# gMLP and SwiGLU layer: x loaded into y's rows, mod_w of g2 read in the v step, LN1 spread row by row, xT of two blocks as one tile, transposes one u step earlier

## The chip, the core and the metric

One core of a Trainium2 chip runs the whole layer as one program. The metric is the device time of the program in microseconds (us). PE is the matrix engine, DVE the vector engine, ACT the scalar engine, POOL the general engine; SP is the sequencer that issues nearly all DMA transfers of this kernel, one after the other, each when its waits are met. A kernel's time is the median of its runs. A bank is one PSUM bank, 128 partitions x 512 float32.

## The reference

One layer on x of 2048 rows x 1024 columns, float32:

```python
mod = silu(c) @ mod_w + mod_b                      # sh1, sc1, g1, sh2, sc2, g2: 1024 numbers each
h   = x * (1 + sc1) + sh1
u, v = split(gelu(h @ w_in + b_in), 2)             # 1024 columns each
v   = layer_norm(v)                                # times ln_g, plus ln_b
sv  = einsum('gts,bnsgc->bntgc', w_s * tril, v) + b_s   # within chunks of 128 rows, 8 groups of columns
x   = layer_norm(2 ** 0.25 * x + (1 + g1) * ((u * sv) @ w_out))           # LN1
h   = x * (1 + sc2) + sh2
g, u = split(h @ ffn_w_in, 2)                      # 2816 columns each
x   = layer_norm(2 ** 0.25 * x + (1 + g2) * ((silu(g) * u) @ ffn_w_out))  # LN2
```

## The kernel before

The 2048 rows are four blocks of 512 (TB), each of four tiles of 128 rows (NT). `mixer(sb)` takes blocks 2sb and 2sb+1 through the first half of the layer; it runs twice. Then `ffn_in(0)`, `ffn_in(1)` and `ffn_out` do the second half. Every float32 operand of a large product is split by `parts` (L91) into a rounded value, which ACT writes (L94), and a remainder, which DVE writes (L95); three matmuls (`HL`) make one product.

A mixer has three steps. **v** (L307 to L324): 384 matmuls of 128x512 for v, in two passes of 8 banks over 8 k steps; with each k step of the first pass `h_piece` loads the rows of x transposed (`xT`, two tiles of 128x512, one a block) and scales them; `wv_piece` loads the weight into a buffer of pool `xs`. The two passes end in sums into `vrow`, eight tiles of pool `late`. **u** (L376 to L383): 8 steps of 48 matmuls; step i also runs the jobs listed for ("u", i), and some of the spatial products (L359). **y** (L439 to L460): a Strassen form of the output product, seven products of 4 k steps of 12 matmuls, 336 in all, in the order 1, 2, 6, 5, 7, 3, 4. Each k step needs a left operand (`y_S`, in the 8 buffers of pool `hB`) and a right one (`y_T`, a 512 KB load from DRAM into the 6 buffers of pool `w`, L404). `evacuate` adds the banks up in `rows`, eight tiles of `late`: `with_x` (L410) loads a half row tile of x, 256 KB, into `xs` and DVE computes ALPHA x + bank (L415). `norm` (L431) then does LN1 of a block: four multiplications by ln1g (L434), the root on POOL (L183), four by 1/std plus ln1b (L435), and a store to DRAM (`x1d`). `norm(0)` stands at the end of product 3; `norm(1)`, of the second block, is run by the caller: for the first mixer in step ("v", 0, 0) of the second, for the second between the products of `ffn_in(0)`.

The u steps of the second mixer carry the *tails* of the first: `tail_load` reads x1d back (`x1c`, pool `late`), PE transposes it (`h2T`, L483), `h2_part` makes up to five operands of it, and `hop` stores put them into DRAM (L475). Tail i is the job of step ("u", i), so tail 7 belongs to the last u step. `load_ops` (L512) reads such operands for `ffn_in`: A11 and A12 in `following`, after the last u step, S1 and S2 after the mixer, S3, A22 and S4 inside `ffn_in`. Products 1, 2, 5, 6, 7, 4, 3 of `ffn_in` need A11, A12, S1, S2, S3, A22, S4 in turn; their weights (`f_0g_b` and so on, L543) go through `parts` as `f_0g_w`.

`mods(to, k, plus)` gives eight jobs `mod_col`: load a 512 KB tile of mod_w (`modw`, pool `lt`, 3 buffers), one DVE pass with a sum (L119), one small addition. sh2 and sc2 are read in steps ("v", 1, d) of the second mixer, g2 in its u steps 6 and 7. `spread` (L139) writes the eight columns of g2 to a line in DRAM, 4 bytes apiece (`g_bc_line`), and loads it back onto all partitions.

The order of each engine's instructions is fixed when the program is built: the tile framework schedules them by a model of time (L906), so a job may come earlier or later than where the code names it. On the chip each engine runs its list in that order.

Of the kernel before, what the change touches and what calls it, by code (L numbers as in the profile page):

```python
# [37 lines left out]
def gmlp_swiglu_layer(  # L38
# [237 lines left out]
    def mixer(sb, jobs, u_done):  # L276
# [8 lines left out]
        def h_piece(d):  # L285
            if sc1[d] is None:
                mod_of(sh1, 0, d, 0.0, "lt")()
                mod_of(sc1, 1, d, 1.0, ("lc", "bc")[d % 2])()
            for x, b in enumerate(blocks):
                r = new("lt" if sb else "u", f"xT{b}_{d}", HALF)  # L290
                nc.sync.dma_start(out=r, in_=xT[d, :, b * TB : (b + 1) * TB])
                nc.scalar.activation(r, r, AF.Identity, bias=sh1[d], scale=sc1[d])
                h[x][d] = parts(r, f"h{b}_{d}", ("hA", "hB")[x])

        def wv_piece(y, k):
            r = new("xs", f"wv{sb}_{y}{k}_raw", HALF)
# [107 lines left out]
            nc.sync.dma_start(out=w.bitcast(F32), in_=wot[B_OF[pr]][k])  # L404
            return w

        rows = [[new("late", f"r{b}_{t}") for t in range(NT)] for b in blocks]
        sts = [[stats_tile(f"ln1_{b}_{t}") for t in range(NT)] for b in blocks]

        def with_x(x, t, cs, ps):  # L410

            xt = new("xs", f"x{blocks[x]}_{t}{cs.start}", HALF)
            row = blocks[x] * TB + t * P
            nc.sync.dma_start(out=xt, in_=inp_x[row : row + P, cs])
            nc.vector.scalar_tensor_tensor(out=rows[x][t][:, cs], in0=xt, scalar=ALPHA, in1=ps, op0=ALU.mult, op1=ALU.add)  # L415

        def evacuate(pr, j, ps):
            if pr in (1, 6, 7, 4):
# [9 lines left out]
                if p == pr:  # L428
                    bn(rows[x][j], sts[x][j], y)

        def norm(x):  # L431
            for t, (mu, rs, nm) in enumerate(norms_of(sts[x], f"ln1_{blocks[x]}")):
                r = rows[x][t]
                nc.vector.scalar_tensor_tensor(out=r, in0=r, scalar=mu, in1=env["ln1g"], op0=ALU.subtract, op1=ALU.mult)  # L434
                nc.vector.scalar_tensor_tensor(out=r, in0=r, scalar=rs, in1=env["ln1b"], op0=ALU.mult, op1=ALU.add)  # L435
                nc.sync.dma_start(out=x1d[blocks[x]][t * P : (t + 1) * P, :], in_=r)
# [2 lines left out]
        order = (1, 2, 6, 5, 7, 3, 4)  # L439
        made = ahead([lambda pr=pr, k=k: (left_y(pr, k), right_y(pr, k)) for pr in order for k in range(NK)], 3)  # L440
        z = None
        for pr in order:
            if pr in (1, 2, 5):
                ps = [bank(f"y{sb}_{pr}_{j}") for j in range(4)]
                if pr == 1:
                    chain = ps
                if pr == 5:
                    z = ps
            ps = chain if pr in (1, 6, 7, 4) else z if pr == 3 else ps
            for k in range(NK):  # L450
                a, w = next(made)
                for j in range(4):
                    for part, wpart in HL:
                        nc.tensor.matmul(  # L454
                            ps[j], lhsT=a[:, part, j * P : (j + 1) * P], rhs=w[:, wpart, :],
                            start=(k == 0 and part == 0 and wpart == 0 and pr in (1, 2, 5)), stop=(k == NK - 1 and part == 1),
                            skip_group_check=True,
                        )
            for j in range(4):
                evacuate(pr, j, ps)  # L460
            if pr == 3:
                norm(0)
# [325 lines left out]
    def mods(to, k, plus):  # L788
        return [mod_of(to, k, d, plus) for d in range(ND)]
# [20 lines left out]
        jobs["u", k + 1] = [wo_prep(k)]  # L810
    jobs["u", 6] = [rows_of_ln1]
    norm = mixer(0, jobs, lambda: None)
    jobs = {("v", 0, 0): [norm]}
    for d, f in enumerate(zip(mods(sh2, 3, 0.0), mods(sc2, 4, 1.0))):
        jobs["v", 1, d] = f
    x1s = {}

    def x1_ahead(i):
        x1s[i] = tail_load(i // 4, i % 4, "late")

    jobs["v", 1, 6] += (lambda: x1_ahead(0),)
    for i in range(2 * NK):
        jobs["u", i] = [lambda i=i: tail(i // 4, i % 4, "lt", ["xs", "lt"], x1s[i])]
        if i < 2 * NK - 1:
            jobs["u", i].append(lambda i=i: x1_ahead(i + 1))
    jobs["u", 6] += mods(g2, 5, 1.0)[:NK]
    jobs["u", 7] += mods(g2, 5, 1.0)[NK:]

    def following():
        early.close()  # L830
        env["ops"] = phase("right", opsA11=(4, UNIT), opsA12=(4, UNIT), raw2=(4, ROW), hr=(1, UNIT))
        ops.update(load_ops(0, ("A11", "A12")))

# [76 lines left out]
```

## Time and profile before

| what | us |
|---|---|
| median of 3 runs | 1896.32 (1894.59 to 1896.58) |
| profiled execution, its own time | 1897.97 |
| its span in the trace | 1896.3 |
| PE busy | 1829.6 (96%) |
| DVE busy | 1251.6 (66%) |
| ACT busy | 687.5 (36%) |
| POOL busy | 513.7 (27%) |

In the trace the first mixer runs to 294 us, the second from 300 to 606, `ffn_in` from 607 to about 1475, `ffn_out` from there to the end. In a row of a timeline the number in brackets is the idle time of the engine before the first of the instructions and what ended it; "xN" is how many instructions of one kind follow each other.

### The profile page before, as it was taken

What the parts mean: (1) busy time and instruction counts of PE and PEld (TensorE: products, weight loads), DVE (VectorE), ACT (ScalarE), POOL (GpSimd) and SP (SyncE); (2) the same over time, 40 slices, a digit from 0 to 9 for tenths busy, and PEclk for the clock granted to TensorE, in tenths of its full rate; (3) what the DMA queues carried; (4) which work ended last, traced back from release to release, by engine and by line L of the source; (5) the groups of instructions that cost most, each with busy time, mean ns of one, the idle gap of its engine ahead of it and who ended that gap; (6) DMA issues with size and microseconds to landing.
All of it is one profiled execution on the core that took longest, in us unless ns stands there. A gap on an engine that the chain in (4) does not pass through costs nothing.

```text
span 1896.3 us, 23225 instructions
## 1 busy us (share of the span) xinstructions
PE 1829.6 (96%) x8168; PEld 1513.0 (80%) x8168; DVE 1251.6 (66%) x1785; ACT 687.5 (36%) x1132; POOL 513.7 (27%) x327
## 2 busy tenths in 40 slices
PE   7999998999977999999999999999999999999997
PEld 5888877888755788888888888888888888888886
DVE  7658759555966776776765656677766344455858
ACT  4254324163421344543333333333334333333320
POOL 0000001001110465576444653555453000000104
PEclk9999999999988999999999999999999999999998
DMA  9638667536988846753567646445645665556532
GB/s 380 198 125 309 199 217 275 195 121 223 366 298 241 309 168 227 260 189 140 192 202 275 237 139 210 167 161 187 207 167 184 211 194 189 183 167 190 173 120 100
DMA packets 173319, 393.24 MB, mean 207 GB/s; under 512 B 20209, under 2 KB 36625, under 8 KB 173202
## 3 DMA queue, kind: packets, MB, share of 16 engines
q1 hardware_dynamic: 173138, 391.73, 59.8%
q8 instruction: 64, 1.05, 0.2%
q14 instruction: 53, 0.43, 0.1%
q0 software_dynamic: 64, 0.03, 0.0%
HBM read 266.11 MB, written 125.58 MB: 207 GB/s over the span
## 4 chain that ended last, share of the span: by engine, by line
PE 86%; DVE 4%; issue 4%; DMA 3%; ACT 1%; POOL 0%; SPq 0%; DVEq 0%; ACTq 0%; POOLq 0%
PE o L672 21%; PE u_ps L348 8%; PE v_ps L314 8%; PE y L454 4%; PE s_ps L359 1%; PE f_4g_X L530 1%; PE f_3g_X L530 1%; PE f_5g_X L530 1%; PE f_2g_X L530 1%; PE f_2u_X L530 1%; PE f_1u_X L530 1%; PE f_4u_X L530 1%; PE f_3u_X L530 1%; PE f_5u_X L530 1%; PE f_6g_X L530 1%
## 5 line engine op out<-in xcount | busy, mean ns | idle before, releaser
L672 PE MATMUL o<-wd_w,alw 128*128 128x512 f32 x1848 | 419.2, 389 | 0.0
L672 PEld LDWEIGHTS o<-wd_w,alw 128*128 128x128 f32 x1848 | 346.8, 188 | 72.0
L314 PE MATMUL v_ps<-wv,h 128*128 128x512 f32 x768 | 179.7, 397 | 19.3 <-ACT h L94 12.5
L183 POOL TENSOR_TENSOR ln_rss<-ln_ves,mhalf 128x4 f32<-128x4 f32 x7 | 16.5, 2359 | 641.9 <-DVE ln_ves L182 641.9
L314 PEld LDWEIGHTS v_ps<-wv,h 128*128 128x128 f32 x768 | 147.1, 192 | 51.5 <-ACT h L94 12.9
L454 PE MATMUL y<-y_T,y_S 128*128 128x512 f32 x672 | 161.8, 403 | 24.0 <-DVE r L415 12.4
L348 PE MATMUL u_ps<-h,wu 128*128 128x512 f32 x768 | 180.4, 394 | 1.4 <-ACT wu L94 1.4
L454 PEld LDWEIGHTS y<-y_T,y_S 128*128 128x128 f32 x672 | 130.7, 196 | 54.3 <-DVE r L415 13.3
L348 PEld LDWEIGHTS u_ps<-h,wu 128*128 128x128 f32 x768 | 144.4, 190 | 31.8 <-ACT wu L94 2.1
L95 DVE TENSOR_TENSOR alw<-al,alw 128x512 fp32r<-128x512 f32 x154 | 100.4, 687 | 87.2 <-ACT alw L94 87.2
L94 ACT CAST alw<-al 128x512 fp32r<-128x512 f32 x154 | 89.0, 620 | 140.9 <-PE o L672 138.8
L95 DVE TENSOR_TENSOR wd_w<-wdl,wd_w 128x512 fp32r<-128x512 f32 x77 | 53.0, 690 | 68.1 <-ACT wd_w L94 68.1
L94 ACT CAST wd_w<-wdl 128x512 fp32r<-128x512 f32 x77 | 47.7, 622 | 106.4 <-PE o L672 78.3
L119 DVE SCALAR_TENSOR_TENSOR modw<-modw,cact 128x1024 f32<-128x1024 f32 x48 | 58.4, 1220 | 14.1 <-DMA modw<-in_modwT 13.9
L94 ACT CAST y_S<-u 128x512 fp32r<-128x512 f32 x48 | 29.0, 621 | 84.2 <-PE y L454 56.7
L95 DVE TENSOR_TENSOR y_S<-u,y_S 128x512 fp32r<-128x512 f32 x48 | 34.7, 734 | 29.2 <-ACT y_S L94 29.1
L495 POOL TENSOR_TENSOR h<-h 128x512 f32<-128x512 f32 x8 | 11.9, 1486 | 146.3 <-DMA x1c<-x1d 54.0
L95 DVE TENSOR_TENSOR wu<-wu_raw,wu 128x512 fp32r<-128x512 f32 x32 | 21.3, 688 | 43.8 <-ACT wu L94 43.8
L626 DVE TENSOR_TENSOR wd<-wd,g_bc 128x512 f32<-128x512 f32 x44 | 36.7, 857 | 13.4 <-DMA wd<-in_wd 12.9
L183 POOL TENSOR_TENSOR lnv_rss<-lnv_ves,mhalf 128x4 f32<-128x4 f32 x4 | 4.3, 1098 | 147.3 <-DVE lnv_mvs L180 81.1
L94 ACT CAST wv<-wv_raw 128x512 fp32r<-128x512 f32 x32 | 19.8, 618 | 67.3 <-DMA wv_raw<-in_wv 43.5
L94 ACT CAST wu<-wu_raw 128x512 fp32r<-128x512 f32 x32 | 18.7, 619 | 57.1 <-PE v_ps L314 36.3
(625 smaller groups left out, 3732.6 us busy)
## 6 DMA issues: line engine op xcount, KB each, us to landing
al<-aop SPq DMA_DIRECT2D x154, 256.0 KB, 2.9
modw<-in_modwT SPq DMA_DIRECT2D x48, 512.0 KB, 6.0
aop<-aop_s SPq DMA_DIRECT2D x88, 256.0 KB, 2.0
y_T<-woT SPq DMA_DIRECT2D x32, 512.0 KB, 4.6
h2S<-hop SPq DMA_DIRECT2D x32, 512.0 KB, 9.7
y_T<-woB SPq DMA_DIRECT2D x24, 512.0 KB, 4.6
h2A<-hop SPq DMA_DIRECT2D x24, 512.0 KB, 8.2
wd<-in_wd SPq DMA_DIRECT2D x44, 256.0 KB, 4.0
```

The costliest lines, as they stand in the source:

```text
L94: nc.scalar.copy(out=o[:, 0, :], in_=src)
L95: nc.vector.tensor_tensor(out=o[:, 1, :], in0=src, in1=o[:, 0, :].bitcast(F32), op=ALU.subtract)
L119: nc.vector.scalar_tensor_tensor(out=w, in0=w, scalar=1.0, in1=env["cact"], op0=ALU.mult, op1=ALU.mult, accum_out=modc[:, j : j + 1],)
L183: nc.gpsimd.tensor_tensor(out=rs, in0=ve, in1=mhalf.broadcast_to([P, m]), op=ALU.pow)
L314: nc.tensor.matmul(ps[x][t], lhsT=h[x][k][:, part, t * P : (t + 1) * P], rhs=w[:, wpart, :], start=(k == 0 and part == 0 and wpart == 0), ...
L348: nc.tensor.matmul(p, lhsT=w[d // 4][:, wpart, (d % 4) * P : (d % 4 + 1) * P], rhs=h[x][d][:, part, :], start=(d == 0 and wpart == 0 and p ...
L359: nc.tensor.matmul(p[:, t * P : (t + 1) * P], lhsT=vrow[x, t][:, ts_], rhs=env["wm"][:, ts_], start=True, stop=True,)
L454: nc.tensor.matmul(ps[j], lhsT=a[:, part, j * P : (j + 1) * P], rhs=w[:, wpart, :], start=(k == 0 and part == 0 and wpart == 0 and pr in ( ...
L495: nc.gpsimd.tensor_tensor(out=a22, in0=a21, in1=a22, op=ALU.add)
L530: nc.tensor.matmul(ps, lhsT=w[:, wpart, k * P : (k + 1) * P], rhs=a[k][:, part, :], start=(first and k == 0 and wpart == 0 and part == 0), ...
L626: nc.vector.tensor_tensor(out=b, in0=b, in1=env["g2"][:, cs], op=ALU.mult)
L672: nc.tensor.matmul(ps[:, cs], lhsT=a[:, part, p * P : (p + 1) * P], rhs=w[:, wpart, cs], start=(first and part == 0 and wpart == 0), stop= ...
```

## The change

- `h_piece` of the second mixer loads xT of both blocks as one tile of 128x1024, in pool `lt`, and scales it with one ACT instruction.
- `x_rows` loads whole row tiles of x, 512 KB each, straight into `rows`; `with_x` computes ALPHA x + bank in place. Pool `xs` is no longer used for x. The code places the first block's rows ahead of product 1 and the second's ahead of product 5.
- `norm` does one row tile at a time. The first mixer's eight calls are spread over steps ("v", 0, 0) to ("v", 0, 7) of the second; the second mixer's first block is still done after product 3, its second block's four tiles between products 1, 2, 5 and 6 of `ffn_in(0)`.
- g2's mod_w is read in steps ("v", 1, d) with sh2 and sc2, three tiles a step.
- Tail 3 joins tail 2 in u step 2; tails 4 to 7 run in u steps 3 to 6. The last u step has none.
- A11 and A12 are loaded ahead of products 5 and 7 of y.

```diff
@@ h_piece
+            if sb:
+                r = new("lt", f"xT{sb}_{d}")
+                nc.sync.dma_start(out=r, in_=xT[d, :, 2 * sb * TB : 2 * (sb + 1) * TB])
+                nc.scalar.activation(r, r, AF.Identity, bias=sh1[d], scale=sc1[d])
             for x, b in enumerate(blocks):
-                r = new("lt" if sb else "u", f"xT{b}_{d}", HALF)
-                nc.sync.dma_start(out=r, in_=xT[d, :, b * TB : (b + 1) * TB])
-                nc.scalar.activation(r, r, AF.Identity, bias=sh1[d], scale=sc1[d])
-                h[x][d] = parts(r, f"h{b}_{d}", ("hA", "hB")[x])
+                if sb:
+                    rx = r[:, x * TB : (x + 1) * TB]
+                else:
...
+                h[x][d] = parts(rx, f"h{b}_{d}", ("hA", "hB")[x])
@@ y step
-        rows = [[new("late", f"r{b}_{t}") for t in range(NT)] for b in blocks]
+        rows = [[], []]
+        def x_rows(x):
+            for t in range(NT):
+                r = new("late", f"r{blocks[x]}_{t}")
+                row = blocks[x] * TB + t * P
+                nc.sync.dma_start(out=r, in_=inp_x[row : row + P, :])
+                rows[x].append(r)
         def with_x(x, t, cs, ps):
-            xt = new("xs", f"x{blocks[x]}_{t}{cs.start}", HALF)
-            row = blocks[x] * TB + t * P
-            nc.sync.dma_start(out=xt, in_=inp_x[row : row + P, cs])
-            nc.vector.scalar_tensor_tensor(out=rows[x][t][:, cs], in0=xt, scalar=ALPHA, in1=ps, op0=ALU.mult, op1=ALU.add)
+            o = rows[x][t][:, cs]
+            nc.vector.scalar_tensor_tensor(out=o, in0=o, scalar=ALPHA, in1=ps, op0=ALU.mult, op1=ALU.add)
@@
-        def norm(x):
-            for t, (mu, rs, nm) in enumerate(norms_of(sts[x], f"ln1_{blocks[x]}")):
+        norms = {}
+        def norm(x, t):
+            if t == 0:
+                norms[x] = norms_of(sts[x], f"ln1_{blocks[x]}")
+            for mu, rs, nm in norms[x][t : t + 1]:
@@
+        x_rows(0)
         for pr in order:
+            also("y", pr)
+            if pr == 5:
+                x_rows(1)
...
-            if pr == 3:
-                norm(0)
-        return lambda: norm(1)
+            if pr == 3 and sb:
+                for t in range(NT):
+                    norm(0, t)
+        return [[lambda x=x, t=t: norm(x, t) for t in range(NT)] for x in range(2)]
@@ jobs of the second mixer
-    jobs = {("v", 0, 0): [norm]}
-    for d, f in enumerate(zip(mods(sh2, 3, 0.0), mods(sc2, 4, 1.0))):
+    jobs = {("v", 0, d): [f] for d, f in enumerate(norm[0] + norm[1])}
+    for d, f in enumerate(zip(mods(sh2, 3, 0.0), mods(sc2, 4, 1.0), mods(g2, 5, 1.0))):
@@
-        jobs["u", i] = [lambda i=i: tail(i // 4, i % 4, "lt", ["xs", "lt"], x1s[i])]
+        step = jobs.setdefault(("u", i if i < 3 else i - 1), [])
+        step.append(lambda i=i: tail(i // 4, i % 4, "lt", ["xs", "lt"], x1s[i]))
...
-    jobs["u", 6] += mods(g2, 5, 1.0)[:NK]
-    jobs["u", 7] += mods(g2, 5, 1.0)[NK:]
@@
-        ops.update(load_ops(0, ("A11", "A12")))
-
+
+    jobs["y", 5] = [lambda: ops.update(load_ops(0, ("A11",)))]
+    jobs["y", 7] = [lambda: ops.update(load_ops(0, ("A12",)))]
@@ ffn_in(0)
-    between[0, 1] = lambda: ops.update(load_ops(0, ("S3", "A22")))
-    between[0, 5] = norm
-    between[0, 6] = lambda: ops.update(load_ops(0, ("S4",)))
+    between[0, 1] = lambda: (norm[1][0](), ops.update(load_ops(0, ("S3", "A22"))))
+    between[0, 2] = norm[1][1]
+    between[0, 5] = norm[1][2]
+    between[0, 6] = lambda: (norm[1][3](), ops.update(load_ops(0, ("S4",))))
```

What this does to the lists of instructions is seen at three places. The first is SP's list around the end of the first mixer's y (`x_30` is a half row tile of x, `xT_n` are tiles of x transposed, `wv_0n_raw` the second mixer's weights). Before:

```order
L404 DMA y_T_2600<-woT_3_335 128x1024
L291 DMA xT_3_2777<-in_xT 128x512
L291 DMA xT_3_2783<-in_xT 128x512
L291 DMA xT_4_2818<-in_xT 128x512
L291 DMA xT_4_2824<-in_xT 128x512
L291 DMA xT_5_2859<-in_xT 128x512
L291 DMA xT_5_2865<-in_xT 128x512
L414 DMA x_30_2662<-in_x 128x512
L297 DMA wv_00_raw<-in_wv 128x512
L291 DMA xT_6_2900<-in_xT 128x512
L297 DMA wv_01_raw<-in_wv 128x512
```

Now, with `wv_00_raw`, `wv_01_raw` and `wv_02_raw` some 50 rows higher, around the first `y_T` of this step:

```order
L411 DMA y_T_2531<-woT_2_334 128x1024
L291 DMA xT_3_2707<-in_xT 128x1024
L411 DMA y_T_2556<-woT_3_335 128x1024
L291 DMA xT_4_2748<-in_xT 128x1024
L304 DMA wv_03_raw<-in_wv 128x512
L291 DMA xT_5_2789<-in_xT 128x1024
L304 DMA wv_04_raw<-in_wv 128x512
```

The first three weights of v no longer stand behind a load of x that waits for an `xs` buffer. The second place is SP's list early in the second mixer's y. Before, from its seventh `y_T` on (`hop` stores and `h2a` loads are those of tails 6 and 7):

```order
L475 DMA hop_2_0_146<-h2S_0_2p 128x1024
L118 DMA modw_4208<-in_modwT 128x1024
L404 DMA y_T_4514<-woB_2_326 128x1024
L404 DMA y_T_4549<-woB_3_327 128x1024
L404 DMA y_T_4566<-woT_0_340 128x1024
L404 DMA y_T_4583<-woT_1_341 128x1024
L118 DMA modw_4212<-in_modwT 128x1024
L118 DMA modw_4216<-in_modwT 128x1024
L475 DMA hop_3_0_116<-h2A_0_3p 128x1024
L404 DMA y_T_4600<-woT_2_342 128x1024
```

Now, again from the seventh `y_T` on:

```order
L411 DMA y_T_4450<-woB_2_326 128x1024
L421 DMA r_0_4376<-in_x 128x1024
L421 DMA r_1_4378<-in_x 128x1024
L421 DMA r_2_4380<-in_x 128x1024
L421 DMA r_3_4382<-in_x 128x1024
L411 DMA y_T_4477<-woB_3_327 128x1024
L421 DMA r_0_4630<-in_x 128x1024
L421 DMA r_1_4632<-in_x 128x1024
L421 DMA r_2_4634<-in_x 128x1024
L421 DMA r_3_4636<-in_x 128x1024
L565 DMA f_0g_b_5008<-in_wf 128x1024
L411 DMA y_T_4494<-woT_0_340 128x1024
```

The loads of mod_w and the stores of tail 7 have left this stretch; the rows of x of both blocks stand in it instead, and behind the ninth `y_T` three more tiles of FFN weights, the tenth and eleventh `y_T`, g2's line and two S operands, before the twelfth. The third place is DVE's list where `ffn_in` begins (`r_n` are rows, `f_0g_w` the remainder of its first weight). Before:

```order
L435 SCALAR_TENSOR_TENSOR r_0_4411<-r_0_4411,ln_2_rss,ln1b_bc 128x1024
L435 SCALAR_TENSOR_TENSOR r_1_4412<-r_1_4412,ln_2_rss,ln1b_bc 128x1024
L435 SCALAR_TENSOR_TENSOR r_2_4413<-r_2_4413,ln_2_rss,ln1b_bc 128x1024
L435 SCALAR_TENSOR_TENSOR r_3_4414<-r_3_4414,ln_2_rss,ln1b_bc 128x1024
L415 SCALAR_TENSOR_TENSOR r_3_4418<-x_30_5031,y_1_3_4451 128x512
L148 BN_STATS ln_3_2_st<-r_2_4417 128x6
L180 BN_AGGR ln_3_mvs<-ln_3_1_st 128x2
L434 SCALAR_TENSOR_TENSOR r_0_4415<-r_0_4415,ln_3_mvs,ln1g_bc 128x1024
L148 BN_STATS ln_3_3_st<-r_3_4418 128x6
L180 BN_AGGR ln_3_mvs<-ln_3_2_st 128x2
L95 TENSOR_TENSOR f_0g_w_5084<-f_0g_b_5080,f_0g_w_5084 128x512
```

Now:

```order
L428 SCALAR_TENSOR_TENSOR r_0_4630<-r_0_4630,y_1_0_4384 128x512
L189 SCALAR_TENSOR_TENSOR ln_2_nms<-ln_2_mvs,ln_2_rss 128x4
L452 SCALAR_TENSOR_TENSOR r_0_4376<-r_0_4376,ln_2_rss,ln1b_bc 128x1024
L452 SCALAR_TENSOR_TENSOR r_1_4378<-r_1_4378,ln_2_rss,ln1b_bc 128x1024
L452 SCALAR_TENSOR_TENSOR r_2_4380<-r_2_4380,ln_2_rss,ln1b_bc 128x1024
L452 SCALAR_TENSOR_TENSOR r_3_4382<-r_3_4382,ln_2_rss,ln1b_bc 128x1024
L428 SCALAR_TENSOR_TENSOR r_1_4632<-r_1_4632,y_1_1_4385 128x512
L148 BN_STATS ln_3_0_st<-r_0_4630 128x6
L428 SCALAR_TENSOR_TENSOR r_2_4634<-r_2_4634,y_1_2_4386 128x512
L428 SCALAR_TENSOR_TENSOR r_3_4636<-r_3_4636,y_1_3_4387 128x512
L95 TENSOR_TENSOR f_0g_w_5012<-f_0g_b_5008,f_0g_w_5012 128x512
```

The four passes of LN1 still stand in one row; the second block's multiplications by ln1g have moved behind the first weights of `ffn_in`.

## Rows read from the trace of the kernel before

**Rows 1.** The page: span, and PE's busy time with its share.

```profile
span 1896.3 us, 23225 instructions
PE 1829.6 (96%) x8168; PEld 1513.0 (80%) x8168; DVE 1251.6 (66%) x1785; ACT 687.5 (36%) x1132; POOL 513.7 (27%) x327
```

**Rows 2.** Chain of waits inside ffn_in, undisturbed: start, us, what.

```profile
675.92 2.72 PE f_1g_X L530 x12
```

**Rows 3.** PE timeline, end of the first y and second v: start, us, operation.

```profile
272.05 22.00 PE L454 MATMUL y<-y_T,y_S 128*128 128x512 f32 x96 [1.74 <-DVE r L83]
300.34 90.05 PE L314 MATMUL v_ps<-wv,h 128*128 128x512 f32 x384 [6.28 <-ACT wv L94]
```

**Rows 4.** SP timeline around 295 us.

```profile
294.81 0.33 SPq L414 DMA_DIRECT2D x<-in_x  x1
295.88 0.33 SPq L297 DMA_DIRECT2D wv_raw<-in_wv  x1
```

**Rows 5.** PE timeline of the second mixer's y.

```profile
498.95 13.86 PE L454 MATMUL y<-y_T,y_S 128*128 128x512 f32 x60
516.23 1.61 PE L454 MATMUL y<-y_T,y_S 128*128 128x512 f32 x6 [3.42 <-DMA y_T<-woB]
519.11 9.65 PE L454 MATMUL y<-y_T,y_S 128*128 128x512 f32 x30 [1.27 <-ACT h L484]
538.40 5.88 PE L454 MATMUL y<-y_T,y_S 128*128 128x512 f32 x18 [9.64 <-DVE r L415]
547.08 30.50 PE L454 MATMUL y<-y_T,y_S 128*128 128x512 f32 x126 [2.79 <-DVE r L415]
582.69 23.59 PE L454 MATMUL y<-y_T,y_S 128*128 128x512 f32 x96 [5.10 <-DMA y_T<-woB]
```

**Rows 6.** DVE timeline before PE's longest wait.

```profile
535.11 2.04 DVE L95 TENSOR_TENSOR h2S_3p<-h2a,h2S_3p 128x512 fp32r<-128x512 f32 x2 [4.97 <-ACT h2S_3p L94]
537.67 0.68 DVE L415 SCALAR_TENSOR_TENSOR r<-x,y 128x512 f32<-128x512 f32 x1
```

**Rows 7.** Busy time by stretch: stretch, us, five engines, granted clock, DMA share, GB/s.

```profile
300.00:390.00 90.00, 89.66 (x383) 73.98 (x384) 61.93 (x115) 20.74 (x32) 3.11 (x1) 0.97 0.60 216
500.00:505.00 5.00, 5.00 (x24) 4.14 (x23) 5.00 (x9) 0.62 (x1) 0.00 (x0) 1.00 1.03 416
575.00:580.00 5.00, 2.58 (x12) 1.81 (x10) 2.49 (x4) 1.14 (x2) 0.00 (x0) 1.00 0.91 76
```

**Rows 8.** The y_T loads from 478 to 545 us.

```profile
DMA to landing us min/median/max: 3.4/6.9/10.7
```

**Rows 9.** SP timeline, the last store of tail 6.

```profile
502.93 0.32 SPq L475 DMA_DIRECT2D hop<-h2S_2p  x1
```

**Rows 10.** PE timeline where ffn_in begins.

```profile
606.99 0.73 PE L530 MATMUL f_0g_X<-h2A,f_0g_w 128*128 128x512 f32 x2 [0.71 <-ACT f_0g_w L94]
614.34 1.22 PE L530 MATMUL f_0u_X<-h2A,f_0u_w 128*128 128x512 f32 x2 [6.62 <-DVE ln_mvs L180]
642.16 2.88 PE L530 MATMUL f_0g_X<-h2S,f_0g_w 128*128 128x512 f32 x12
```

**Rows 11.** DVE timeline where ffn_in begins.

```profile
608.17 4.87 DVE L435 SCALAR_TENSOR_TENSOR r<-r,ln_rss,ln1b_bc 128x1024 f32<-128x1024 f32 x4
612.95 0.68 DVE L415 SCALAR_TENSOR_TENSOR r<-x,y 128x512 f32<-128x512 f32 x1
616.12 0.64 DVE L95 TENSOR_TENSOR f_0g_w<-f_0g_b,f_0g_w 128x512 fp32r<-128x512 f32 x1
617.88 1.77 DVE L95 TENSOR_TENSOR f_0u_w<-f_0u_b,f_0u_w 128x512 fp32r<-128x512 f32 x1
```

**Rows 12.** modw from 300 to 370 us: count, duration min/median/max, first and last start.

```profile
L119 DVE SCALAR_TENSOR_TENSOR modw<-modw,cact x16: 1216/1222/1226, 317.7 to 362.2; 128x1024 f32<-128x1024 f32 x16
DMA to landing us min/median/max: 3.2/5.3/6.3
```

**Rows 13.** SP's waits from 480 to 640 us, for g2's line.

```profile
SPq L144 <- DMA g_bc_line<-modc: 9.0, 1, 9.0
```

More of the change, by code (lines that the diff above doesn't have):

```diff
@@ L288, in h_piece @@
                 mod_of(sc1, 1, d, 1.0, ("lc", "bc")[d % 2])()
+            if sb:
+                r = new("lt", f"xT{sb}_{d}")
+                nc.sync.dma_start(out=r, in_=xT[d, :, 2 * sb * TB : 2 * (sb + 1) * TB])
+                nc.scalar.activation(r, r, AF.Identity, bias=sh1[d], scale=sc1[d])
             for x, b in enumerate(blocks):
-                r = new("lt" if sb else "u", f"xT{b}_{d}", HALF)
-                nc.sync.dma_start(out=r, in_=xT[d, :, b * TB : (b + 1) * TB])
-                nc.scalar.activation(r, r, AF.Identity, bias=sh1[d], scale=sc1[d])
-                h[x][d] = parts(r, f"h{b}_{d}", ("hA", "hB")[x])
+                if sb:
+                    rx = r[:, x * TB : (x + 1) * TB]
+                else:
+                    rx = new("u", f"xT{b}_{d}", HALF)
+                    nc.sync.dma_start(out=rx, in_=xT[d, :, b * TB : (b + 1) * TB])
+                    nc.scalar.activation(rx, rx, AF.Identity, bias=sh1[d], scale=sc1[d])
+                h[x][d] = parts(rx, f"h{b}_{d}", ("hA", "hB")[x])
         def wv_piece(y, k):
@@ L822, in gmlp_swiglu_layer @@
     for i in range(2 * NK):
-        jobs["u", i] = [lambda i=i: tail(i // 4, i % 4, "lt", ["xs", "lt"], x1s[i])]
+        step = jobs.setdefault(("u", i if i < 3 else i - 1), [])
+        step.append(lambda i=i: tail(i // 4, i % 4, "lt", ["xs", "lt"], x1s[i]))
         if i < 2 * NK - 1:
-            jobs["u", i].append(lambda i=i: x1_ahead(i + 1))
-    jobs["u", 6] += mods(g2, 5, 1.0)[:NK]
-    jobs["u", 7] += mods(g2, 5, 1.0)[NK:]
+            step.append(lambda i=i: x1_ahead(i + 1))
     def following():
```

## The prediction

> **What bounds the kernel now.** I read the page first: PE is busy 1829.6 of 1896.3 us [rows 1]. So a change that takes no matmul away can gain only what PE waits, and what its matmuls lose by running slower than elsewhere. The measure of "slower" is the chain of waits in an undisturbed part of `ffn_in`: 12 matmuls in 2.72 us, 0.2267 us each [rows 2]. The change touches the time from the end of the first mixer's y to the first tiles of `ffn_in`; in the lists of all engines nothing moves behind that. So the second view is PE's timeline of that stretch, and three places in it lose time against this pace.
>
> (a) Ahead of v of the second mixer PE idles 6.28 us (294.05 to 300.34), ended by ACT's part of the first weight, and the 384 matmuls behind take 90.05 us where 384 x 0.2267 = 87.05 [rows 3]; the granted clock in this stretch is 0.97 [rows 7]. Lost: 6.28 + 3.0 = 9.3. SP's timeline says why the weight was late: it was issued at 295.88, right behind a load of x at 294.81 [rows 4] that waits for an `xs` buffer.
>
> (b) y of the second mixer runs from 498.95 to 582.69 + 23.59 = 606.28: 107.3 us for 336 matmuls, which at pace take 76.2. Lost: 31.1, of which the bracketed idle times are 3.42 + 1.27 + 9.64 + 2.79 + 5.10 = 22.2; the other 8.9 are slower matmuls behind the gaps (30 in 9.65 where the pace gives 6.8) [rows 5]. That is 0.4 us on top of each idle us. The 9.64 is DVE's sum L415: it came at 537.67, in order behind the remainders of tail 7, which had themselves waited 4.97 for ACT [rows 6]. The 5.10 is a `y_T` behind g2's line, whose 4-byte pieces kept the DMA engines 0.91 busy at 76 GB/s [rows 7]; SP waited 9.0 us for that line [rows 13].
>
> (c) From 606.28 to 642.16 `ffn_in` does 96 matmuls in 35.9 us instead of 21.8: lost 14.1 [rows 10]. DVE's timeline shows the first weight's remainder only at 616.12, behind four passes of LN1 (4.87) and a sum at 612.95 that frees an `xs` buffer [rows 11].
>
> Together 54.5 us: the most that this change can give.
>
> **The change, part by part.** *(a)* `wv_00` to `wv_02` are issued some 50 rows earlier and x no longer passes through `xs`, so the 6.28 goes, and its echo in the clock. What is late next: DVE's last four sums of y, which free the banks of v's first pass; PE reaches these banks with about 0.3 us to spare by my count, and two remainders that need xT loads stand between. I take 1 us left, bounds 0 to 4 (the idle time now and its echo, halved). Gain 9.3 - 1.0 = 8.3.
>
> *(b)* Tail 7 and the loads of mod_w leave the stretch, and the sums no longer wait for loads that are issued late. The 9.64, 2.79, 1.27 and the 5.10 lose their causes. What is late next is `y_T`, since the rows of x, 16 x 256 KB as 8 x 512 KB, now stand ahead of its eighth and ninth. The queue is full there: 416 GB/s [rows 7], so 512 KB take 1.26 us; the slowest landing is 10.7 us [rows 8], which means about eight transfers in flight. I count in order from the last store of tail 6, issued at 502.93 [rows 9]; in the new list the seventh `y_T` stands in that place. The eighth is 5 transfers on, issued at 509.2, landed some 10 us later at 519.2; the ninth 6 on, 526.7; the tenth 4 on, 531.7; the eleventh 532.9; the twelfth and thirteenth 4 on each, 537.9 and 542.9. PE wants the n-th at 498.95 + 2.72 (n - 1), plus the waits so far: the eighth at 518.0 (wait 1.2), the ninth at 521.9 (4.8), the tenth at 529.4 (2.3), the twelfth at 537.1 (0.8), the thirteenth at 540.6 (2.3). Idle 11.4, with 0.4 on top for the clock 16.0: y takes 76.2 + 16.0 = 92.2 instead of 107.3. Gain 15.1, bounds 0 (the loads are late by as much as now) and 31.1 (no wait at all).
>
> The trace has 416 GB/s there [rows 7], for loads from and stores to DRAM. The Trainium skill (DMA: Bandwidth & Descriptors, Where 436 GB/s comes from) holds that about 358 GB/s of the DRAM side bind such transfers. By that an estimate is 1.46 us for 512 KB and waits of 18.1 instead of 11.4, and the kernel would end near 1874; the trace speaks against it, so the sum goes by the row.
>
> *(c)* At y's end T, DVE's list has the last sums, the four passes of LN1 (4.87), three more sums at 0.68, statistics, then four weights' remainders in a row. From the end of the passes at T + 3.4 the first is done near T + 6.4, instead of 616.76 - 606.28 = 10.5 now; the next three at 1.77 each [rows 11] at T + 11.7. With some 1.1 for the statistics that stand near them and 2.72 for the last twelve matmuls, 48 matmuls end at T + 15.5 instead of 10.9. Lost 4.6, with the echo of 0.4 some 6.4; gain 14.1 - 6.4 = 7.7, bounds 3 (the passes hold the first weight as now) and 9.
>
> *Costed at nothing.* Eight more mod_w tiles in v: 8 x 1.22 on DVE [rows 12] is 10 us beside 61.93 busy of 90 while PE sets the pace, and 4.2 MB on a DMA share of 0.60 [rows 7]; without that cover they cost rival 3. The tails are the same instructions one u step earlier, under 48 matmuls a step (10.9 us); without that cover, u steps would show gaps as y does. xT as one tile is the same bytes; the single ACT instruction comes ahead of both blocks' parts. LN1 row by row leaves its four passes in one row on DVE in the second mixer, so I give that edit nothing there; in v the passes lie under the same cover as mod_w.
>
> Sum: 8.3 + 15.1 + 7.7 = 31.1. The profiled execution took 1897.97, 1.65 above the median of 1896.32. 1897.97 - 31.1 = 1866.9, less 1.65: **1865**.
>
> **The rivals.** 1. The `y_T` loads keep their whole loss: the rows of x, FFN weights and S operands ahead of them cost as much as tail 7 did. Only (a) and (c) gain, 16.0: 1880. For it: the queue is at 416 GB/s where 13 new transfers enter; against: 4.2 MB of mod_w and the line have gone from there. 2. No wait at all in y, because the queue drains earlier than I count (tail 7's stores are all out before): the whole 31.1 of (b), 1849. 3. **Slower:** in v 24 mod_w tiles pass through the three `lt` buffers. Now 16 run 2.97 us apart (317.7 to 362.2), with 5.3 to landing [rows 12]. A buffer's turn is landing plus 1.22, so three buffers give a tile each (landing + 1.22)/3 = s. From 310 on the last is issued at 310 + 23 s; g2's line follows (9.0 of wait [rows 13]) and behind it the load of tail 2's rows (10.7 [rows 8]), which PE wants near 406. So it bites from s = 3.3 on. At landings of 10.7, s = 4.0 and PE stands 15 us: 1880. It is slower than before only if the loss passes 31, from s = 4.7, a landing of 12.8, above all I see: about 1900 at s = 4.8. 4. The change doesn't do what it says: the loads go out no earlier than now since their buffers come free no earlier, and the gaps of y come back under other names: 1896.
>
> **How the numbers follow.** The forecast .74; rival 1 .08; rival 2 .11; rival 3 on the slower side .04; rival 4 .03. The forecast's own bounds, with (a) at 5.3 to 9.3, (b) at 8 to 25 and (c) at 3 to 9, are about 1853 to 1880. The range adds most of rival 1 and half of rival 2: 1850 to 1882; rivals 3 and 4 stay outside. A change of 0.2%, 3.8 us, is about what a measurement of this kernel can tell from none. Faster by more .93, within .03, slower .04.
>
> **What would show it.** In the profile after: PE's idle time ahead of v under 4 us and its 384 matmuls in about 87; y of the second mixer near 92 us, its waits named `y_T` and lying between the eighth and the thirteenth, none of them ended by a sum of DVE; the first weight's remainder some 6 us behind y's end, `ffn_in`'s first 96 matmuls in some 28; u steps of 48 matmuls without new gaps; nothing changed from the second tile of `ffn_in` on. It is wrong if waits in y are ended by something else or sum to under 5 or over 18 us, if u waits for tails or g2's line, or if v shows gaps ended by mod_w or `vrow`.

## The result, and the profile after

The changed kernel takes 1867.97 us (median of 4 runs, 1862.81 to 1869.08) against 1895.45 before: ratio 0.9851, 95% interval 0.983 to 0.9871. The forecast was 1865. The page after, its first lines:

```profile
span 1867.4 us, 23186 instructions
PE 1825.5 (98%) x8168; PEld 1511.0 (81%) x8168; DVE 1249.9 (67%) x1785; ACT 683.9 (37%) x1124; POOL 515.3 (28%) x327
```

The span is 28.9 us shorter, and of the matmuls' busy time only 4 us went: what went was waiting. PE's timeline of the same places as [rows 3, 5, 10] (start, us, operation, in brackets the idle time before and what ended it):

```profile
271.20 22.04 PE L475 MATMUL y<-y_T,y_S 128*128 128x512 f32 x96 [0.60 <-DVE r L83]
293.08 87.20 PE L321 MATMUL v_ps<-wv,h 128*128 128x512 f32 x384
...
488.87 19.34 PE L475 MATMUL y<-y_T,y_S 128*128 128x512 f32 x84
511.41 4.58 PE L475 MATMUL y<-y_T,y_S 128*128 128x512 f32 x12 [3.19 <-DMA y_T<-woB]
518.88 14.21 PE L475 MATMUL y<-y_T,y_S 128*128 128x512 f32 x48 [2.89 <-DVE ln_st L148]
535.08 23.64 PE L475 MATMUL y<-y_T,y_S 128*128 128x512 f32 x96 [1.99 <-DMA y_T<-woT]
560.48 22.04 PE L475 MATMUL y<-y_T,y_S 128*128 128x512 f32 x96 [1.76 <-DVE r L428]
...
589.60 4.14 PE L552 MATMUL f_0g_X<-h2A,f_0g_w 128*128 128x512 f32 x10 [4.08 <-DVE f_0g_w L95]
...
611.92 2.88 PE L552 MATMUL f_0g_X<-h2S,f_0g_w 128*128 128x512 f32 x12
...
657.76 2.88 PE L552 MATMUL f_1g_X<-h2A,f_1g_w 128*128 128x512 f32 x12
```

The 6.28 us ahead of v are gone, and v takes 87.20. y runs from 488.87 to 560.48 + 22.04 = 582.52, 93.65 us (107.33 before), in five pieces with 9.83 us of idle time between them. The first 96 matmuls of `ffn_in` take 611.92 - 582.52 = 29.40 (35.88 before). The last row is a mark that every run below has: the last twelve matmuls of `f_1g_X`. It stands 75.24 us behind y's end. In the kernel before it is this row, 80.36 behind 606.28:

```profile
686.64 2.88 PE L530 MATMUL f_1g_X<-h2A,f_1g_w 128*128 128x512 f32 x12
```

There the changed kernel is 28.88 us ahead, and it stays so to the end. All of the difference lies between 270 and 690 us, in four pieces: 0.81 by the end of the first mixer's y, 9.30 to the start of u (its matmuls start at 380.12, 390.23 before), 13.68 in y, 5.12 from there to the mark, less 0.03 in u.

### The profile page after: what moved, and what is told of

It reads as the page before. It is cut to its first block, busy times and chain, and to the rows that moved or that the text cites. A ratio compares the mean times of both kernels' runs of the same rounds, so it can differ in the third digit from the quotient of the medians.

```text
span 1867.4 us, 23186 instructions
## 1 busy us (share of the span) xinstructions
PE 1825.5 (98%) x8168; PEld 1511.0 (81%) x8168; DVE 1249.9 (67%) x1785; ACT 683.9 (37%) x1124; POOL 515.3 (28%) x327
## 4 chain that ended last, share of the span: by engine, by line
PE 88%; issue 5%; DVE 3%; DMA 1%; ACT 1%; POOL 0%; SPq 0%; DVEq 0%; POOLq 0%; ACTq 0%
PE o L694 21%; PE v_ps L321 9%; PE u_ps L355 8%; PE y L475 4%; PE s_ps L366 1%; PE f_4g_X L552 1%; PE f_5g_X L552 1%; PE f_3g_X L552 1%; PE f_2g_X L552 1%; PE f_4u_X L552 1%; PE f_3u_X L552 1%; PE f_2u_X L552 1%; PE f_5u_X L552 1%; PE f_1u_X L552 1%; PE f_10u_X L552 1%
## 5 line engine op out<-in xcount | busy, mean ns | idle before, releaser
L655 DVE TENSOR_TENSOR wd<-wd,wd 128x512 f32<-128x512 f32 x44 | 30.2, 687 | 7.8 <-DMA wdB<-wd 7.4
## 6 DMA issues: line engine op xcount, KB each, us to landing
modw<-in_modwT SPq DMA_DIRECT2D x48, 512.0 KB, 5.5
y_T<-woT SPq DMA_DIRECT2D x32, 512.0 KB, 4.2
h2S<-hop SPq DMA_DIRECT2D x32, 512.0 KB, 9.9
y_T<-woB SPq DMA_DIRECT2D x24, 512.0 KB, 5.2
h2A<-hop SPq DMA_DIRECT2D x24, 512.0 KB, 8.8
```

The costliest lines, as they stand in the source:

```text
L655: nc.vector.tensor_tensor(out=o, in0=a, in1=b, op=ALU.subtract)
```

## Experiments

Each run is the changed kernel with one edit or up to three. Their profiled executions are compared by three lengths read from PE's timeline as above: the wait ahead of v, y (first matmul to the end of the last), and y's end to the mark.

**The wait ahead of v.** The first mixer's x through `xs` again:

```diff
@@ x_rows and with_x, for the first mixer only
-                nc.sync.dma_start(out=r, in_=inp_x[row : row + P, :])
...
+                xt = new("xs", f"x{blocks[x]}_{t}{cs.start}", HALF)
...
+                nc.sync.dma_start(out=xt, in_=inp_x[row : row + P, cs])
```

> The changed kernel, but the first mixer's y loads x in half row tiles through pool xs again (the second mixer keeps whole row tiles). In its list the first weight of the second mixer's v stands behind the last of those x loads again. Theory, that this queueing made the wait ahead of v: PE idles 5 to 7 us ahead of v, ended by ACT's part of that weight, the 384 matmuls take about 90 us, and the time is 9 us above the changed kernel's 1868, about 1877. Rival, that the one-tile xT or the spread LN1 removed the wait: no idle time ahead of v, about 1868.

1880.74 us (ratio to before 0.9919, interval 0.9894 to 0.9945). PE's timeline, and SP's ahead of it:

```profile
300.31 14.75 PE L321 MATMUL v_ps<-wv,h 128*128 128x512 f32 x56 [5.58 <-ACT wv L94]
```

```profile
294.18 0.33 SPq L432 DMA_DIRECT2D x<-in_x  x1
295.62 0.33 SPq L304 DMA_DIRECT2D wv_raw<-in_wv  x1
```

The time is 4 us above the 1877 that I expected. The wait is back with its old releaser, and SP issues the weight behind the load of x again, as in [rows 4]. From y's end to u's start it takes 8.11 us more than in the changed kernel, and 1.5 more in the y ahead of it. So x through `xs` makes that wait, and neither the one-tile xT nor the spread LN1, which both stayed, takes it away. (2.7 us more went behind the second y, with a wait of 2.20 for an operand A22.)

What holds the weight is a buffer of its own. On DVE in the kernel before:

```profile
295.17 0.69 DVE L415 SCALAR_TENSOR_TENSOR r<-x,y 128x512 f32<-128x512 f32 x1
```

This sum ends at 295.86, and SP, whose last wait (0.7 us) is put down to it, issues the weight at 295.88; in the run such a sum ends at 295.59 and the weight goes out at 295.62. So the weight's own buffer of `xs` comes free only when DVE has added up the x tile that holds it.

**The three edits to the second mixer.** Its x through `xs` (as above, with `sb`), the tails in their own u steps, g2's mod_w in the u step, each undone alone:

```diff
@@ tails
-        step = jobs.setdefault(("u", i if i < 3 else i - 1), [])
+        step = jobs.setdefault(("u", i), [])
@@ g2
-    for d, f in enumerate(zip(mods(sh2, 3, 0.0), mods(sc2, 4, 1.0), mods(g2, 5, 1.0))):
+    for d, f in enumerate(zip(mods(sh2, 3, 0.0), mods(sc2, 4, 1.0))):
...
+    jobs["u", 6] += mods(g2, 5, 1.0)[:NK]
+    jobs.setdefault(("u", 7), []).extend(mods(g2, 5, 1.0)[NK:])
```

> The changed kernel, but the second mixer's y loads x in half row tiles through pool xs again (the first mixer keeps whole row tiles). Its y_T loads no longer stand behind eight rows of x, but the sums of product 1 wait for x tiles issued behind the tenth and eleventh y_T. Theory, that rows of x trade waits for sums against waits for y_T: PE idles some 9 us ahead of product 6, ended by a sum of DVE, the eighth to thirteenth y_T cost nothing, y takes 95 to 98 us, and f_0g_w comes 2 us later: about 1873. Rival, that loading x into the rows carried the whole gain in y: y takes 107 us again, about 1881.

> The changed kernel, but tails 3 to 7 run in u steps 3 to 7 as before. Theory, that tail 7 in the last u step cost y time twice, on DVE ahead of the sums and on the queue: y takes 98 to 102 instead of 93.7 us, with a wait ended by DVE again and a y_T wait at the seventh tile, where the first four rows of x stand now: about 1874. Rival 1, that the tail alone made the 9.64 us wait and all that followed: y near 107, about 1881. Rival 2, that it was hidden and the x tiles alone made the wait: 1868.

> The changed kernel, but g2's mod_w is read in u steps 6 and 7 as before; its eight loads stand among the y_T loads again, three tiles of FFN weights move behind the 26th y_T in exchange, and the line of g2 comes late in y. Theory, that 4.2 MB more in a full queue and the line cost y time: the eighth y_T 2 to 3 us later, a wait behind the line, y takes 97 to 101 us: about 1873. Rival, that g2's loads replace the weights' one for one and the line finds the queue idle: y as in the changed kernel, about 1868.

All three expectations of a loss fell: 1867.24, 1863.74 and 1867.49 us, none slower than the changed kernel, and each with a *shorter* y (table below). With x through `xs` the wait at the eighth `y_T` vanishes. Its y in PE's timeline, and where the gain went again:

```profile
489.99 16.58 PE L480 MATMUL y<-y_T,y_S 128*128 128x512 f32 x72
...
516.18 1.15 PE L480 MATMUL y<-y_T,y_S 128*128 128x512 f32 x3 [2.34 <-DMA y_T<-woT]
...
550.85 22.04 PE L480 MATMUL y<-y_T,y_S 128*128 128x512 f32 x96 [0.55 <-DVE r L83]
```

```profile
PE f_0u_X L557 <- DVE ln_mvs L180: 5.7, 1, 5.7
PE f_0g_X L557 <- ACT f_0g_w L94: 3.5, 2, 2.8
```

y takes 82.90, 10.75 less than the changed kernel; the nine us of waiting for sums that I expected did not come. But from y's end to the mark it is 82.15, 6.9 more: in `ffn_in` weights wait for statistics again (the second fence is PE's waits: waiter, releaser, total, times, longest). Loading x into the rows of the second mixer is an exchange of one for the other.

So two of the edits were undone together.

> Two edits undone at once that cost nothing when undone alone: the second mixer's x goes through pool xs again, and tails 3 to 7 run in u steps 3 to 7. Now the remainders of tail 7 stand on DVE ahead of all sums of product 1, and the x tiles of these sums behind tail 7's stores on the queue. Theory, that it takes this pair to make y's long wait: y takes 97 to 107 us with a wait of over 7 us ended by a sum of DVE, about 1882. Rival, that g2's loads are needed for it: no wait ended by a sum is over 3 us, y takes 83 to 90, about 1868.

> Two edits undone at once: tails 3 to 7 in u steps 3 to 7 and g2's mod_w in u steps 6 and 7; the second mixer's x stays in whole rows, so product 1's sums stand ahead of tail 7's remainders or wait for nothing that tail 7 holds up. Theory, that sums behind the tail made y's long wait: y takes 88 to 95 us, waits named y_T, about 1866. Rival, that tail and mod_w together on the queue made it: y 103 us or more, about 1879.

> Two edits undone at once: the second mixer's x through pool xs and g2's mod_w in u steps 6 and 7; the tails stay one u step early. Theory, that without tail 7 nothing holds up the sums of product 1 for long, and g2's loads and line cost a y_T wait or two: y takes 86 to 93 us, about 1872. Rival, that x in half tiles among g2's loads makes the long wait by itself: a wait of over 7 us ended by a sum, y 97 us or more, about 1882.

1871.02, 1866.79 and 1866.78 us. The first pair does bring a long wait behind a sum; the others do not:

```profile
518.93 5.22 PE L480 MATMUL y<-y_T,y_S 128*128 128x512 f32 x15 [8.08 <-DVE r L433]
```

But y is 91.50 there and not 97 to 107, since its other waits come to only 4.0 us. The sum did not come late for the reason I had given, either: in that run the last remainder of tail 7 is done at 512.0, DVE has nothing left to do by 513.2 and stands idle for 4.91 us until the sum's x has landed, at 518.14. With tails and g2 undone y is 92.63, as expected, but its longest wait, 6.28, is for a scaling of tail 7 on ACT and not for a `y_T`; with x and g2 undone y is 84.31, below the 86 to 93 that I expected. Last, all three:

> The three edits to the second mixer undone at once: its x through pool xs, tails 3 to 7 in u steps 3 to 7, g2's mod_w in u steps 6 and 7. The first mixer's x, the xT tiles and the loads of A11 and A12 stay as changed. Theory, that the 107 us of y need all three at once, since each alone and two pairs gave 83 to 93: y takes 103 to 109 us, with a wait of over 7 us ended by a sum of DVE and one behind g2's line; with 82 from y's end to the end of f_1's X (as in the run with x through xs) the time is about 1887. Rival, that the earlier loads of A11 and A12 took the rest out of y: y takes 90 to 97 us, about 1875.

1887.21 us (0.9958, 0.9943 to 0.9973), as the theory had it; the earlier loads of A11 and A12, which stayed, did not take the rest out of y. Here the gaps of [rows 5] are back in PE's timeline. On DVE the sum stands behind tail 7's remainders, as in [rows 6], but what it waits for last, 0.99 us, is its x:

```profile
507.38 2.13 PE L480 MATMUL y<-y_T,y_S 128*128 128x512 f32 x6 [3.24 <-DMA y_T<-woB]
...
528.62 6.04 PE L480 MATMUL y<-y_T,y_S 128*128 128x512 f32 x18 [8.90 <-DVE r L433]
537.18 28.88 PE L480 MATMUL y<-y_T,y_S 128*128 128x512 f32 x126 [2.52 <-DVE r L433]
570.23 25.22 PE L480 MATMUL y<-y_T,y_S 128*128 128x512 f32 x96 [4.17 <-DMA y_T<-woB]
```

```profile
523.48 2.04 DVE L95 TENSOR_TENSOR h2S_3p<-h2a,h2S_3p 128x512 fp32r<-128x512 f32 x2 [1.80 <-ACT h2S_3p L94]
...
527.88 0.69 DVE L433 SCALAR_TENSOR_TENSOR r<-x,y 128x512 f32<-128x512 f32 x1 [0.99 <-DMA x<-in_x]
```

All eight combinations of the three edits (us; one profiled execution each, the median of 4 or 5 runs):

| undone | y | y's end to the mark | median |
|---|---|---|---|
| none | 93.65 | 75.24 | 1867.97 |
| x through xs | 82.90 | 82.15 | 1867.24 |
| tails | 89.97 | 72.97 | 1863.74 |
| g2 | 89.73 | 76.08 | 1867.49 |
| x and tails | 91.50 | 81.31 | 1871.02 |
| x and g2 | 84.31 | 79.88 | 1866.78 |
| tails and g2 | 92.63 | 74.89 | 1866.79 |
| all three | 105.17 | 80.39 | 1887.21 |
| (kernel before) | 107.33 | 80.36 | 1895.45 |

The long y needs all three undone. Any one edit shortens it, by 12 to 21 us, and with the other two in, each of the three makes y longer. The mark tells another thing: it comes 4 to 8 us later in each row with x through `xs` than in the same row without, whatever else is undone. That part of the gain hangs on x in the rows of the second mixer. (Two other runs have the second mixer of the changed kernel: that with the first mixer undone has 93.89 and 77.93, that with a tile of 16 bytes more, below, 92.73 and 74.46. So y repeats within 1.2 us and the mark within 3.5; the differences of 4 us rest on one execution each.)

**Rows ahead of y_T: the queue, or the bytes?**

```diff
@@ x_rows
-                nc.sync.dma_start(out=r, in_=inp_x[row : row + P, :])
+                (nc.scalar if sb else nc.sync).dma_start(out=r, in_=inp_x[row : row + P, :])
```

> The changed kernel, but the eight loads of x rows of the second mixer are issued by ACT instead of SP, so that no y_T stands behind them on SP's queue; the bytes and the time at which they can start are the same. Theory, that y_T waits because it stands behind rows in one queue: the waits at the eighth and thirteenth y_T go, y takes 83 to 87 us, about 1859. Rival, that the DMA engines are full there whoever issues: the rows take the same share, the y_T land as late, y takes 92 to 95 us, 1866 to 1870.

1867.59 us, y 487.34 to 579.13, 91.79: the rival, but for 0.2 us of y. PE's timeline, ACT's, and the busy time of 496 to 502 us (stretch, us, PE, weight loads, DVE, ACT, POOL, granted clock, DMA share, GB/s):

```profile
509.47 7.49 PE L475 MATMUL y<-y_T,y_S 128*128 128x512 f32 x24 [5.23 <-DMA y_T<-woB]
519.42 12.95 PE L475 MATMUL y<-y_T,y_S 128*128 128x512 f32 x48 [2.46 <-DMA y_T<-woT]
```

```profile
495.65 11.64 ACTq L421 DMA_DIRECT2D r<-in_x  x6
507.33 1.66 ACT L94 CAST y_S<-u 128x512 fp32r<-128x512 f32 x3 [13.01 <-DMA r<-in_x]
```

```profile
496.00:502.00 6.00, 6.00 (x28) 4.99 (x27) 3.19 (x6) 0.00 (x0) 0.00 (x0) 1.00 1.02 419
```

The DMA engines were full, 419 GB/s, and a second queue did not give `y_T` more of them: the first wait stands at the seventh `y_T` now, issued at 494.39, and the slowest `y_T` of this y took 14.9 us to land, against 9.9 in the changed kernel. ACT was held up 11.64 us in issuing six loads, with its casts behind them. So what must go from ahead of these `y_T` is bytes; the next run does that.

**A version that takes the better of both.** Only the sums of the first block wait early in y, and only the last rows, of the second block, stand at the start of `ffn_in`. So the first block's x goes through `xs`, the second's into the rows:

```diff
@@ x_rows and with_x
-                nc.sync.dma_start(out=r, in_=inp_x[row : row + P, :])
+                if not (sb and x == 0):
+                    nc.sync.dma_start(out=r, in_=inp_x[row : row + P, :])
...
+            if sb and x == 0:
+                xt = new("xs", f"x{blocks[x]}_{t}{cs.start}", HALF)
...
+                nc.sync.dma_start(out=xt, in_=inp_x[row : row + P, cs])
```

> The changed kernel, but the second mixer's first block loads x in half tiles through pool xs, and only its second block in whole row tiles; these four loads then stand behind the thirteenth y_T instead of ahead of the ninth. Theory, that rows of x ahead of the eighth and ninth y_T cost y 10 us, and that the last sums through xs cost the start of ffn_in 7: y takes 82 to 87 us and the first 96 matmuls of ffn_in 29 to 30, about 1858. Rival, that the two cannot be had together, since the last half tiles for product 6 come late: 1866 to 1868.

1857.46 us (0.9804, 0.9788 to 0.9821), 10.5 below the changed kernel, whose interval begins at 0.983. PE's timeline:

```profile
489.59 23.05 PE L480 MATMUL y<-y_T,y_S 128*128 128x512 f32 x99
514.95 0.94 PE L480 MATMUL y<-y_T,y_S 128*128 128x512 f32 x3 [2.31 <-DMA y_T<-woT]
...
551.03 22.01 PE L480 MATMUL y<-y_T,y_S 128*128 128x512 f32 x96 [0.59 <-issue]
...
576.68 3.90 PE L557 MATMUL f_0g_X<-h2A,f_0g_w 128*128 128x512 f32 x10 [1.83 <-DVE f_0g_w L95]
...
643.97 2.88 PE L557 MATMUL f_1g_X<-h2A,f_1g_w 128*128 128x512 f32 x12
```

y is 83.45, as expected, and the mark comes 70.93 behind its end, earlier than in any row of the table; the first 96 matmuls of `ffn_in` take 26.4 us where I expected 29 to 30. LN1's four passes end 0.6 us behind y's end here and 4.1 behind it in the changed kernel, and the first weight is waited for 1.83 us instead of 4.08; why DVE comes to these passes earlier is open. It is the fastest of all kernels run.

**LN1's passes behind the first weights.** LN1 of the second mixer's first block is called behind product 1 of `ffn_in(0)` instead of at the end of y, and the factor of its four 1/std passes is made to depend on f_0's first sums:

```diff
@@ norm, for the second mixer's first block
+                        env["late_rs"] = small.tile([P, NT], F32, tag="late_rs", name="late_rs", bufs=1)
+                    late_rs = env["late_rs"][:, t : t + 1]
+                    nc.vector.scalar_tensor_tensor(out=late_rs, in0=env["c1"][:, 0:1], scalar=0.0, in1=rs, op0=ALU.mult, op1=ALU.add)
+                    rs = late_rs
...
-    between[0, 1] = lambda: (norm[1][0](), ops.update(load_ops(0, ("S3", "A22"))))
+    between[0, 1] = lambda: ([f() for f in norm[0]], norm[1][0](), ops.update(load_ops(0, ("S3", "A22"))))
```

> The changed kernel, but the four 1/std passes of the second mixer's first block are made to depend on the first product of ffn_in (their factor is 0 times one of its sums plus the factor), so that DVE has the first weights' remainders ahead of them. Theory, that these passes hold up the first weight: its remainder comes 2 to 3 us behind y's end instead of 6.4, the first 96 matmuls of ffn_in take 24 to 26 us instead of 29.4, and of these 4 to 5 us up to 3 go again in waits for A22, whose buffers come free later: about 1865. Rival, that ACT's part or the load of the weights is what comes late: 96 matmuls in 29 us, 1868 or more.

1887.33 us, slower by 19. PE's timeline in `ffn_in` (y ends at 584.43), and DVE's:

```profile
587.40 2.60 PE L555 MATMUL f_0g_X<-h2A,f_0g_w 128*128 128x512 f32 x10
...
610.49 4.40 PE L555 MATMUL f_0g_X<-h2S,f_0g_w 128*128 128x512 f32 x10 [7.11 <-DVE f_0g_w L95]
```

```profile
603.37 5.86 DVE L458 SCALAR_TENSOR_TENSOR r<-r,late_rs,ln1b_bc 128x1024 f32<-128x1024 f32 x4
609.16 0.68 DVE L604 TENSOR_TENSOR f_0g_c<-f_0g_Y,f_0g_c 128x512 f32<-128x512 f32 x1
609.76 0.67 DVE L95 TENSOR_TENSOR f_0g_w<-f_0g_b,f_0g_w 128x512 fp32r<-128x512 f32 x1
```

The first weight does come at 587.40, 3.0 behind y's end instead of 7.1, so the passes did hold it. But they now hold a later weight for 7.11, and the mark comes 77.62 behind y's end, no earlier than in the changed kernel. Moved to this place, the passes save nothing. From the mark to the end of the span it takes 1223.7 us instead of 1209.6, and in the whole execution PE is busy 17.1 us longer for the same matmuls: they run slower. The edit had brought a new tile of 16 bytes a partition (`late_rs`), so the changed kernel was run with such a tile alone, which nothing reads:

```diff
@@ beside the constants
+    shift = small.tile([P, NT], F32, tag="shift", name="shift", bufs=1)
+    nc.vector.memset(shift, 0.0)
```

> The changed kernel with one more tile of 16 bytes a partition in pool small, written once and not read: the engines' lists are the same but for that write, and all pools on one side lie 16 bytes higher. The run in which LN1's passes were put behind the first weights had such a tile too, and took 14 us more from its f_1 on, where nothing is waited for. Theory, that the address alone slows those matmuls: 1880 to 1885, with ffn_out's long run of 1816 matmuls at about 419 us as there, instead of 411.8. Rival, that the new place of the passes did it by some other way: 1868 and 411.8.

1884.97 us (0.9955, 0.994 to 0.997): the tile alone does it; but for the one write, the engines' lists are those of the changed kernel. The long run of matmuls in `ffn_out`, of this kernel, and of the changed one:

```profile
1452.67 419.12 PE L696 MATMUL o<-wd_w,alw 128*128 128x512 f32 x1816
```

```profile
1443.75 411.79 PE L694 MATMUL o<-wd_w,alw 128*128 128x512 f32 x1816
```

That is 0.2308 instead of 0.2268 us a matmul.

## Why the prediction came out

**(a)** 8.3 was forecast, 9.30 came, all that I had counted as lost, and 0.81 more ahead of it from a smaller gap in the first y [rows 3]. The 1 us that I left for late sums was not needed. The cause, x through `xs`, is shown by the run that undoes it; how it acts is a little other than I read it, since the weight waited for a buffer itself and not only behind a load of x that did.

**(b)** 15.1 forecast, 13.68 measured. The way I counted the new y, by transfers ahead of each `y_T`, held up. SP's timeline:

```profile
495.07 0.65 SPq L411 DMA_DIRECT2D y_T<-woB  x1
496.31 4.02 SPq L421 DMA_DIRECT2D r<-in_x  x4
501.35 0.33 SPq L411 DMA_DIRECT2D y_T<-woB  x1
502.83 3.79 SPq L421 DMA_DIRECT2D r<-in_x  x4
...
508.82 0.33 SPq L411 DMA_DIRECT2D y_T<-woT  x1
```

The seventh, eighth and ninth `y_T` are issued at 495.07, 501.35 and 508.82, 6.3 and 7.5 apart as counted. But the first of them goes out 6.20 us behind y's start and not 3.98 as I had it (502.93 - 498.95), and that is the 2 us by which the eighth comes later. PE waits at the eighth (3.19, counted 1.2), the ninth (2.89, counted 4.8) and the thirteenth (1.99, counted 2.3); the tenth and twelfth, 3.1 together, did not wait. The ninth wait is put down to statistics on DVE that end at 518.79, but its `y_T`, issued at 508.82, landed no earlier than 518.7 by the usual 9.9 (the y_T loads of this y); which of the two held PE is not settled.

```profile
DMA to landing us min/median/max: 3.2/9.9/9.9
```

The rate that I counted with held too (419 and 420 GB/s in the stretches below). The Trainium skill (DMA: Bandwidth & Descriptors, Where 436 GB/s comes from) lets about 358 GB/s bind transfers between DRAM and SBUF; the trace disagrees, with 416 GB/s before and 419 after.

Two sizes were off, one against the other, so that the total came out so near is in part luck. Idle time was 9.83 and not 11.4, and 1.76 of it was ended by a sum of product 7 on DVE, where I had said that no wait would be. And the slower matmuls behind the gaps took 93.65 - 76.2 - 9.83 = 7.6, 0.78 us for each idle one, not 0.4. Busy time by stretch, columns as above:

```profile
511.00:516.00 5.00, 4.58 (x12) 3.40 (x12) 2.87 (x5) 0.00 (x0) 0.00 (x0) 0.66 1.02 419
519.00:524.00 5.00, 5.00 (x12) 3.80 (x13) 0.00 (x0) 0.00 (x0) 0.00 (x0) 0.50 1.03 420
```

Behind the gap of 3.19 the granted clock falls to a mean of 0.66, and behind that of 2.89, some five us later, it is 0.50, the lower of its two levels (1.2 GHz), for a whole stretch: 12 matmuls in 5 us. The 0.4 came from the y before alone, and it is no rate: over the nine rows of the table the slower matmuls cost 0.3 to 0.8 us for each idle one (3.1 for 10.42 with g2 undone, 7.6 for 9.83 here).

What failed in (b) is the reading of why. I gave the 9.64 to DVE's order, the sum standing behind tail 7's remainders. SP's timeline of the kernel before has the load of x for that sum:

```profile
529.70 0.65 SPq L414 DMA_DIRECT2D x<-in_x  x1
```

The loads of x in that stretch took 5.3 to 7.0 us to land, so this one was there at 535.0 at the earliest, and the sum at 537.67 could have come at most 2.7 us sooner had no remainder stood ahead of it. The larger part of the 9.64 was the late load, which I had named only beside it. Ahead of that load SP had waited 4.7 us at a load of mod_w and 3.9 at a store of tail 7; that would explain why both of these edits must be undone, beside x through `xs`, for the long y to come back, but no run takes the two waits apart. And I took tail 7, the mod_w loads and the late sums together, the whole edit as one. The table shows that each of the three edits alone would have brought y to 84 to 93, and that the rows of x, the edit I charged with 16.0, cost 10.75 in y and are paid back 6.9 later. The forecast of y was right, but it credits to three edits together what any one of them does.

**(c)** 7.7 forecast, 6.48 measured to the 96th matmul. DVE's timeline:

```profile
581.70 4.87 DVE L452 SCALAR_TENSOR_TENSOR r<-r,ln_rss,ln1b_bc 128x1024 f32<-128x1024 f32 x4
...
588.87 0.68 DVE L95 TENSOR_TENSOR f_0g_w<-f_0g_b,f_0g_w 128x512 fp32r<-128x512 f32 x1
589.47 0.68 DVE L95 TENSOR_TENSOR f_0u_w<-f_0u_b,f_0u_w 128x512 fp32r<-128x512 f32 x1
```

The first remainder is done 7.0 behind y's end (6.4 forecast). The next take 0.68 and not 1.77, so they set nothing. I had let the fourth one end the stretch; it is the first that does, with ten matmuls of every twelve behind it and a slower clock (10 in 4.14). Then 1.36 of the gain is lost again between the 96th matmul and the mark, where I had said nothing changes. Of this 0.8 is a wait for A22, which takes buffers of `late` that the second block's rows hold until LN1 has stored them:

```profile
PE f_0g_X L552 <- DMA h2A<-hop: 0.8, 2, 0.5
```

The four pairs of the table say that this gain comes from x in the rows of the second mixer.

**Costed at nothing.** mod_w in v: right, its 384 matmuls take 87.20. The tails: right, u is longer by 0.03. LN1 row by row: right, and more than that: written for whole blocks, the program has the same instructions in the same order on all five engines, so this edit does nothing here. The one-tile xT was not tried alone. None of the rivals came; rival 1's y, 107, is about what undoing all three gives.

## To carry to other kernels

When a stall has several feeders, cost the edits one by one, in every combination if they are few: here each of three edits alone took 12 to 21 us from the same stall, and with the other two in, each cost y some 4 to 11. Where the DMA engines are full, count the bytes that stand ahead of the transfer that PE wants next; another queue did not help here, later loads did. And a gap's price includes the slower matmuls behind it: give that as a range, here 0.3 to 0.8 us for each idle one.

## What the runs showed of the hardware

A tile of 16 bytes a partition that nothing reads made the kernel 0.9% slower: ffn_out's matmuls went from 0.2268 to 0.2308 us each at a granted clock of 1.00, the 384 of v from 87.20 to 88.57, while the 96 that end the first y kept their 22.0. In the built program it moves most tiles by 32 bytes a partition (not 16, as the expectation has it) and leaves the others where they were; nothing else changes. So in this kernel the place of operands sets the pace of a matmul; which operand it is, and why, stays open. It also means that when an experiment allocates something, the pace of matmuls far from the edit must be compared before its time is read.
